# GDN chunk matrices kept in SBUF from preparation to merge, and the second half of the retention's gate columns moved behind the z columns

## The chip, the cores and the metric

The kernel runs on one core of one Trainium2 chip. The metric is the device time of one execution in microseconds (us). The number compared is the median over several runs of each kernel.

## The reference, cut to what matters

One layer of a hybrid block over 1280 tokens (256 context, 1024 latent, width 1024), all in 32-bit floats: modulated RMSNorm, one input projection, two head groups side by side, an output projection, a SwiGLU, a final norm. The part that the change touches:

```python
p = (h @ w_in)                                   # columns: q,k,v (GDN) | z | a,b | rq rk rv rg (retention)
qkv_a = silu(short_conv(qkv_a, conv_w))          # 5 taps, centred
q, k  = l2_normalize(q) * HEAD_DIM**-0.5, l2_normalize(k)
# gated delta rule (GDN), forward and backward, per chunk:
A     = where(strict, einsum('id,jd->ij', kb, kc) * decay, 0)
sol   = triangular_solve(A + I, rhs, lower, unit_diagonal)
qk    = einsum('id,jd->ij', qc, kc) * decay
...
o_gdn = rms_norm(o_f + o_b, gdn_norm_g) * silu(z)
o_ret = head_group_norm(r_f + r_b, ret_norm_g) * silu(rg)
```

The two parts changed are the way in which A's inverse is formed (its tiles are called the chunk matrices here), and the place in the program of half of the product that gives `rg`.

## The kernel before, in words

Every product of the input projection is done three times in a split form (high times high, high times low, low times high). Two forms of it matter here.

- *Token-major products* (`token_major(g, ...)`, tile `tm`, lines 371 to 373): group `g` is 256 columns of weights, 8 tiles of 128 latent tokens, and 8 x 3 matmuls of 128x256 for each tile, so 192 matmuls for a group. Groups 6 and 7 are the two halves of the gate columns `rg`, 8 and 9 those of `z`. A finish on ScalarE (`res`, line 532) makes silu of each bank and a DMA stores it to DRAM (`rd` or `zd`).
- *Convolution blocks* (`conv_block`, tile `b`, lines 605 to 607): 128 columns of q, k or v of one head, in chunks of 512 tokens of 24 matmuls each (and one of 256 for context). ScalarE copies a chunk out twice (`u`, and `y` at line 609); VectorE adds the other four taps (line 615); ScalarE applies silu (line 618).

Around the change the program goes as follows. The four k blocks come first, then norms: on VectorE a chain of small operations ends in `Gr` (line 671), which TensorE turns (`GT`, line 673), and which goes to DRAM as `grow_d`. Then come four q blocks (`qstat`, tile `qt`, turns each), and in the first two of them `ada_rest(5, half)`: a chain of eight VectorE operations over four loads of weights (`acc`, lines 497 and 499), one matmul `gr` (line 504), and one addition (`row`, line 505). Groups 6 and 7 of the token-major product follow, from the pool W2.

Then the GDN preparation. Ten tiles of 128 tokens go in three batches of 4, 4 and 2. `pre(t)` forms k.k (`kk`, line 724) and k.q (`kq`, 729) on TensorE; for each direction it loads a row of decays to all partitions (`gw`), GpSimd masks it (line 736), ScalarE takes four exponentials (740), and VectorE multiplies (`ut` at 744, `sp` at 746). `ut` goes to DRAM (`un`). `invert(b)` reads the 32x32 diagonal blocks back from `un` (`yr`, line 763), and solves all blocks of the batch at once on VectorE with 31 pairs of operations (lines 777 and 779, on `L`, `X` and `tmp`), then turns the result (`XT`, 781) and stores it to DRAM (`xd`). `merge(b)` loads the whole batch of matrices (`U`, line 795, from `un`) and puts the inverted blocks over its diagonal (799) and into `t` (800); TensorE then grows the blocks from 32 to 64 to 128 (tiles `m`, lines 819 to 846).

In program text the order is: solve(0), solve(1), four v blocks (tile `vT`, line 868, turns them; `vt` is stored to `sd`), the preparation of batch 2, merge(0), the load of the table `rope`, invert(2), merge(1), merge(2), and groups 8 and 9. Program text is not the order on the engines: a scheduler sets one order for each engine, with its own estimate of durations and with what the pools' buffers allow, and each engine runs its list strictly in that order. SyncE's queue (SP), which issues most loads and stores, has such a list too, and a transfer that must wait holds all that are behind it. Any edit to buffers or text can so reorder all engines.

Of the kernel before, what the change touches and what calls it, by code (L numbers as in the profile page):

```python
# [8 lines left out]
F32 = mybir.dt.float32  # L9
# [3 lines left out]
ALU = mybir.AluOpType  # L13
# [4 lines left out]
P = 128  # L18
# [4 lines left out]
NTOK = NCTX + NLAT  # L23
TT = NTOK // P
LT = NLAT // P
H = 4
# [12 lines left out]
def build(nc, tc, ap, dbg=None, stop=None, marks=None):  # L39
    root = ExitStack()  # L40
    V, S, G, T, SY = nc.vector, nc.scalar, nc.gpsimd, nc.tensor, nc.sync
# [149 lines left out]
    try:  # L191
# [426 lines left out]
            S.activation(y[:, a0:], y[:, a0:], AF.Silu)  # L618

        def newy():  # L620
            return CV.tile([P, NTOK], F32, tag="y", name="y", bufs=3)

        a4, b4, kds4, neG4 = (sm[n].rearrange("p (t d h) -> p t d h", d=2, h=4) for n in ("ab", "beta", "kds", "neG"))

# [78 lines left out]
        checkpoint("q")  # L703
        token_major(6, LAT, fin_gate, S, W2, SY)
        qstat(H - 1, qys[H - 1])
        token_major(7, LAT, fin_gate, S, W2, SY)
        checkpoint("rg")
        close(R2)
        close(W2)
# [4 lines left out]
        BATCH = [[0,1,2,9],[3,8,4,7],[5,6]]  # L714
        where = {t: (b, c) for b, ch in enumerate(BATCH) for c, t in enumerate(ch)}

        un = [dr.tile([P, 2, len(ch) * H, P], F32, tag="un%d" % b, name="un%d" % b) for b, ch in enumerate(BATCH)]

        def pre(t):
            b, c = where[t]  # L720
            kc = load(GP, kd[t], "kc", 2)
            pk = bank_b("kk")
            for h in range(H):
                T.matmul(pk[:, h * P:(h + 1) * P], kc[:, h, :], kc[:, h, :], start=True, stop=True)
            if t >= 2:
                qc = load(GP, qd[t - 2], "qc", 2)
                pq = bank_b("kq")
                for h in range(H):
                    T.matmul(pq[:, h * P:(h + 1) * P], kc[:, h, :], qc[:, h, :], start=True, stop=True)
            for d in range(2):  # L730
                gw = GP.tile([P, H, P], F32, tag="gw", name="gw", bufs=2)
                SY.dma_start(gw.rearrange("p h i -> p (h i)"),
                             grow_d[c8(t, d), :].rearrange("a b -> (a b)").partition_broadcast(P))
                e = GP.tile([P, H, P], F32, tag="e", name="e", bufs=2)
                sg = 1 if d == 0 else -1
                G.affine_select(out=e, in_=gw, compare_op=ALU.is_ge, fill=FAR, base=0,
                                pattern=[[0, H], [sg, P]], channel_multiplier=-sg)
                for h in range(H):
                    col = t * 8 + d * 4 + h
                    S.activation(e[:, h, :], e[:, h, :], AF.Exp, bias=sm["nG"][:, col:col + 1])  # L740
                if t >= 2:
                    sp = GP.tile([P, H, P], F32, tag="sp", name="sp", bufs=2)
                ut = GU.tile([P, H, P], F32, tag="ut", name="ut", bufs=2)
                V.tensor_tensor(ut.rearrange("p h i -> p (h i)"), pk, e.rearrange("p h i -> p (h i)"), ALU.mult)
                if t >= 2:
                    V.tensor_tensor(sp.rearrange("p h i -> p (h i)"), pq, e.rearrange("p h i -> p (h i)"), ALU.mult)
                SY.dma_start(un[b][:, 1 - d, c * H:(c + 1) * H, :], ut)
                if t >= 2:
                    SY.dma_start(sd[t, :, 8 - 8 * d], sp.rearrange("p h i -> p (h i)"))

# [4 lines left out]
        def invert(b):  # L755

            nc_ = len(BATCH[b])
            nu = nc_ * H
            nb = 4 * nu
            xd = xds[b] = dr.tile([4 * nb, 1024], F32, tag="xd%d" % b, name="xd%d" % b)  # L760
            yr = GI.tile([P, 1024], F32, tag="yr", name="yr", bufs=1)
            for k in range(4):
                SY.dma_start(yr[k:2 * nb:4].rearrange("r (i j) -> r i j", j=32),
                             un[b][q32[k]].rearrange("i e u j -> (e u) i j")[:, :, q32[k]])
            L = GI.tile([P, 1024], F32, tag="L", name="L", bufs=3)
            X = GI.tile([P, 1024], F32, tag="X", name="X", bufs=2)
            G.memset(X, 0.0)
            G.memset(X[:, 0::33], 1.0)
            m = lambda t: t[:2 * nb].rearrange("p (i j) -> p i j", j=32)
            S.activation(L[:nb], yr[:nb], AF.Copy)  # L770
            V.tensor_copy(m(L)[nb:], yr[nb:2 * nb].rearrange("p (i j) -> p j i", j=32))
            for j in range(31):
                n = 31 - j
                tmp = GI.tile([P, 256], F32, tag="tmp%d" % b, name="tmp", bufs=2)
                t3 = tmp[:2 * nb, :n * (j + 1)].rearrange("p (i c) -> p i c", c=j + 1)
                sh = [2 * nb, n, j + 1]
                V.tensor_tensor(t3, bc(m(L)[:, j + 1:, j], sh, 2), bc(m(X)[:, j, :j + 1], sh, 1), ALU.mult)
                xs = m(X)[:, j + 1:, :j + 1]
                V.tensor_tensor(xs, xs, t3, ALU.subtract)
            XT = GI.tile([P, 1024], F32, tag="L", name="XT", bufs=3)  # L780
            V.tensor_copy(m(XT), X[:2 * nb].rearrange("p (i j) -> p j i", j=32))
            for i, x in enumerate((X[:nb], XT[nb:2 * nb], X[nb:2 * nb], XT[:nb])):
                SY.dma_start(xd[i * nb:(i + 1) * nb], x)

        def blocks(b):

            nu = len(BATCH[b]) * H
            nb = 4 * nu

            def blk(dram, k):  # L790
                return dram.rearrange("(u b) (i j) -> b i u j", b=4, j=32)[k]

            at = G2 if b == 1 else GM
            uu = at.tile([P, 2, len(BATCH[b]), H, P], F32, tag="U", name="U%d" % b, bufs=1)
            SY.dma_start(uu.rearrange("p e c h j -> p e (c h) j"), un[b])
            tt = at.tile([P, 2, nu, 64], F32, tag="t64", name="t64", bufs=1)
            G.memset(tt, 0.0)
            for k in range(4):
                SY.dma_start(uu[q32[k]].rearrange("p e c h j -> p (e c h) j")[:, :, q32[k]], blk(xds[b][:2 * nb], k))
                SY.dma_start(tt[q32[k]].rearrange("p e u j -> p (e u) j")[:, :, (k % 2) * 32:(k % 2) * 32 + 32],  # L800
                             blk(xds[b][2 * nb:], k))
            return uu, [uu[:, 1 - d] for d in range(2)], [tt[:, d] for d in range(2)]

        def merge(b):
# [11 lines left out]
            for n in range(nu):  # L816
                for d, p, a, bb in pairs:
                    ca = (a % 2) * 32
                    T.matmul(ps1[q[bb], n * 32:n * 32 + 32], u[d][q[a], n, q[bb]], t[d][q[a], n, ca:ca + 32],
                             start=True, stop=True)  # L820
            xt1 = GM.tile([P, 16, 32], F32, tag="xt1", name="xt1", bufs=1)
            V.tensor_scalar(xt1.rearrange("p n j -> p (n j)")[:, :nu * 32], ps1[:, :nu * 32], -1.0, None, ALU.mult)
            ps2, ps3 = bank_b("m1"), bank_b("m1")
            for n in range(nu):
# [11 lines left out]
            halves = [(0, slice(0, 64), slice(64, 128)), (1, slice(64, 128), slice(0, 64))]  # L836
            for n0 in range(0, nu, 8):
                ps1, ps2 = bank_b("m2"), bank_b("m2")
                xt2 = GM.tile([P, 8, 64], F32, tag="xt2", name="xt2", bufs=1)
                for n in range(8):  # L840
                    for d, A, B in halves:
                        T.matmul(ps1[B, n * 64:n * 64 + 64], u[d][A, n0 + n, B], t[d][A, n0 + n, :], start=True, stop=True)
# [31 lines left out]
        RP = pool("rp", side="right")  # L874
        rope = RP.tile([P, TT, P], F32, tag="rope", name="rope")
        GM = pool("gm", side="right")
        for t in BATCH[2]:
            pre(t)
        close(GP)
# [7 lines left out]
        merge(2)  # L887


        for g in (8, 9):  # L890
            token_major(g, LAT, fin_gate, S, W)
        checkpoint("rgz")
        close(GM)
# [779 lines left out]
```

## Time and profile before

| | us |
|---|---|
| Median of 3 runs | 1485.98 (1479.36, 1485.98, 1486.84) |
| The profiled execution, own time | 1482.3 |
| Its span in the profile | 1480.4 |
| PE (TensorE matmuls) busy | 1399.8 (95%) |
| DVE (VectorE) busy | 981.1 (66%) |
| ACT (ScalarE) busy | 610.5 (41%) |
| POOL (GpSimd) busy | 579.5 (39%) |

The profile shows one execution. "Busy" sums the time in which an engine has an instruction running. PE lacks 80.6 us of the span; the stretch of 40 equal slices shows most of that between 300 and 470 us, and between 600 and 740 us. The stretch that the change touches is 195 to 480 us. The mean granted TensorE clock is 0.981 of full.

In the views, PE is TensorE's matmuls, PEld its weight loads, SP the SyncE queue. "out<-in" names tiles; a bracket at a row's end is the idle time of the engine ahead of it and what ended it. A row of the table by windows has the window, its length, then for PE, PEld, DVE, ACT and POOL the busy time and the count of instructions, then the granted TensorE clock, the mean busy share of the 16 DMA engines, and GB/s.

### The profile page before, as it was taken

What the parts mean: (1) busy time and instruction counts of PE and PEld (TensorE: products, weight loads), DVE (VectorE), ACT (ScalarE), POOL (GpSimd) and SP (SyncE); (2) the same over time, 40 slices, a digit from 0 to 9 for tenths busy, and PEclk for the clock granted to TensorE, in tenths of its full rate; (3) what the DMA queues carried; (4) which work ended last, traced back from release to release, by engine and by line L of the source; (5) the groups of instructions that cost most, each with busy time, mean ns of one, the idle gap of its engine ahead of it and who ended that gap; (6) DMA issues with size and microseconds to landing.
All of it is one profiled execution on the core that took longest, in us unless ns stands there. A gap on an engine that the chain in (4) does not pass through costs nothing.

```text
span 1480.4 us, 24179 instructions
## 1 busy us (share of the span) xinstructions
PE 1399.8 (95%) x8919; PEld 1200.6 (81%) x8919; DVE 981.1 (66%) x1909; ACT 610.5 (41%) x1336; POOL 579.5 (39%) x493
## 2 busy tenths in 40 slices
PE   7999999997889999998799899999999999999997
PEld 2798888876879999898588688877888888788886
DVE  6568797379772535789677886746555554657586
ACT  5543554765222111446444533323333333454454
POOL 0130010220102353254135588999555553335321
PEclk9999999999899999999799999999999999999999
DMA  9537686696878625985633265765232242786863
GB/s 338 186 104 230 178 245 204 199 297 191 256 193 272 247 69 185 411 328 181 217 115 115 85 215 210 266 240 178 107 107 107 107 150 74 239 279 195 306 202 114
DMA packets 170710, 293.95 MB, mean 199 GB/s; under 512 B 43528, under 2 KB 93912, under 8 KB 166496
## 3 DMA queue, kind: packets, MB, share of 16 engines
q1 hardware_dynamic: 119040, 248.98, 49.3%
q10 hardware_dynamic: 49072, 35.83, 7.7%
q0 software_dynamic: 2480, 7.60, 1.4%
q8 instruction: 70, 1.15, 0.3%
q14 instruction: 48, 0.39, 0.1%
HBM read 206.60 MB, written 85.77 MB: 197 GB/s over the span
## 4 chain that ended last, share of the span: by engine, by line
PE 40%; POOL 6%; DMA 2%; issue 1%; DVE 1%; ACT 0%; POOLq 0%; DVEq 0%; ACTq 0%
PE ffn L1362 7%; PE ffn L1360 6%; PE ffn L1361 6%; PE fo L1486 5%; PE fo L1488 5%; PE fo L1487 5%; DMA wd<-tw 2%; PE op L1219 2%; PE op L1220 2%; PE op L1221 2%; POOL ws L1333 1%; POOL tw L1414 1%; POOL tw L1413 1%; POOL tw L1416 1%; POOL tw L1415 1%
## 5 line engine op out<-in xcount | busy, mean ns | idle before, releaser
L371 PE MATMUL tm<-whi,hhi 128*128 128x256 f32 (+1 forms) x704 | 200.8, 290 | 7.2 <-ACT res L532 3.6
L372 PE MATMUL tm<-wlo,hhi 128*128 128x256 f32 (+1 forms) x704 | 200.4, 287 | 1.3 <-DVE wlo L345 1.3
L373 PE MATMUL tm<-whi,hlo 128*128 128x256 f32 (+1 forms) x704 | 198.7, 287 | 0.0
L371 PEld LDWEIGHTS tm<-whi,hhi 128*128 128x128 f32 x704 | 133.9, 192 | 11.5 <-ACT res L532 4.0
L1360 PE MATMUL ffn<-t,whi 128*128 128x512 f32 x352 | 136.9, 390 | 1.3 <-ACT whi L344 1.3
L1362 PE MATMUL ffn<-t,wlo 128*128 128x512 f32 x352 | 137.0, 390 | 0.8 <-DVE wlo L345 0.8
L372 PEld LDWEIGHTS tm<-wlo,hhi 128*128 128x128 f32 x704 | 134.9, 192 | 3.1 <-DVE wlo L345 1.7
L1361 PE MATMUL ffn<-t,whi 128*128 128x512 f32 x352 | 137.0, 389 | 0.0
L344 ACT ACTIVATE whi<-wraw 128x512 fp32r<-128x512 f32 (+2 forms) x98 | 75.1, 770 | 147.9 <-PE ffn L1361 81.9
L373 PEld LDWEIGHTS tm<-whi,hlo 128*128 128x128 f32 x704 | 134.2, 192 | 0.6 <-DVE hlo L314 0.2
L344 ACT ACTIVATE whi<-ws 128x512 fp32r<-128x512 f32 x88 | 55.6, 632 | 172.5 <-PE ffn L1361 131.3
L345 DVE TENSOR_TENSOR wlo<-ws,whi 128x512 fp32r<-128x512 f32 x88 | 94.0, 1069 | 46.5 <-ACT whi L344 46.3
L1486 PE MATMUL fo<-whi,ahi 128*128 128x512 f32 x308 | 119.3, 389 | 0.7 <-ACT ahi L344 0.7
L1487 PE MATMUL fo<-wlo,ahi 128*128 128x512 f32 x308 | 119.9, 389 | 0.0
L1488 PE MATMUL fo<-whi,alo 128*128 128x512 f32 x308 | 119.0, 390 | 0.0
L345 DVE TENSOR_TENSOR wlo<-wraw,whi 128x512 fp32r<-128x512 f32 (+2 forms) x92 | 100.7, 1097 | 23.4 <-ACT whi L344 23.4
L1360 PE MATMUL ffn<-b,whi 128*128 128x512 f32 x264 | 104.1, 394 | 4.1 <-ACT whi L344 4.1
L1362 PE MATMUL ffn<-b,wlo 128*128 128x512 f32 x264 | 103.9, 393 | 0.7 <-DVE wlo L345 0.7
L1361 PE MATMUL ffn<-b,whi 128*128 128x512 f32 x264 | 103.7, 393 | 0.0
L605 PE MATMUL b<-hhi,whi 128*128 128x512 f32 (+1 forms) x256 | 94.7, 370 | 0.8 <-ACT y L609 0.8
L607 PE MATMUL b<-hhi,wlo 128*128 128x512 f32 (+1 forms) x256 | 94.6, 370 | 0.0
L606 PE MATMUL b<-hlo,whi 128*128 128x512 f32 (+1 forms) x256 | 93.8, 366 | 0.0
(451 smaller groups left out, 3422.0 us busy)
## 6 DMA issues: line engine op xcount, KB each, us to landing
adaw<-ada SPq DMA_DIRECT2D x48, 512.0 KB, 4.6
pk<-sd SPq DMA_DIRECT2D x16, 1536.0 KB, 15.1
wraw<-wfi SPq DMA_DIRECT2D x44, 512.0 KB, 4.5
ar<-ad SPq DMA_DIRECT2D x33, 512.0 KB, 4.4
w<-wfo SPq DMA_DIRECT2D x22, 512.0 KB, 3.6
wd<-tw SPq DMA_DIRECT2D x11, 1024.0 KB, 4.9
ad<-act SPq DMA_DIRECT2D x20, 512.0 KB, 3.2
raw<-wd SPq DMA_DIRECT2D x20, 512.0 KB, 4.8
```

Source lines behind the costliest of these rows:

```text
L344: S.activation(hi, raw, AF.Copy)
L345: e.tensor_tensor(lo, raw, hi.bitcast(F32), ALU.subtract)
L371: T.matmul(o, hhi[:, k, tsl], whi[:, k % 4, :], start=(k == 0), stop=False)
L372: T.matmul(o, hhi[:, k, tsl], wlo[:, k % 4, :], start=False, stop=False)
L373: T.matmul(o, hlo[:, k, tsl], whi[:, k % 4, :], start=False, stop=(k == KT - 1))
L605: T.matmul(o, whi[:, k, :], hh, start=(k == 0), stop=False)
L1360: T.matmul(o, whi[:, k, :], xhi(xn, slice(0, 4), k), start=(first and k == 0), stop=False, **kw)
L1361: T.matmul(o, whi[:, k, :], xlo(xn, slice(0, 4), k), start=False, stop=False, **kw)
L1362: T.matmul(o, wlo[:, k, :], xhi(xn, slice(0, 4), k), start=False, stop=(k == 3), **kw)
L1486: T.matmul(po[g][i], ahi[:, ts], whi, start=(j == 0 and not kw), stop=False, **kw)
L1487: T.matmul(po[g][i], ahi[:, ts], wlo, start=False, stop=False, **kw)
L1488: T.matmul(po[g][i], alo[:, ts], whi, start=False, stop=(j == FH - 1), **kw)
```

## The change

- The products of k.k and the decays are written straight into SBUF tiles `us[b]` (`U0` and `U1` in the pool GU, `U2` in GM), in which `merge` then works. The 20 stores `un<-ut` of 256 KB and the three loads `U<-un` (2, 2 and 1 MB) are gone.
- The diagonal blocks go from `us[b]` to a small DRAM tensor `yd` in four transfers, and come back in one load `yr<-yd`; before they came by four loads out of `un`.
- `token_major(7, ...)` moves from behind `qstat` of the last head to the loop at the end, as `for g in (8, 9, 7)`, and takes its weights from the pool W in place of W2.
- Buffers: `y` 3 to 2, `gw` 2 to 3, the tile `e` is gone (the decays are masked and raised in place in `gw`), `L` 3 to 2, `X` 2 to 1, `tmp` shared and single, `xt1` and `xt2` share one buffer.

```diff
-            return CV.tile([P, NTOK], F32, tag="y", name="y", bufs=3)
+            return CV.tile([P, NTOK], F32, tag="y", name="y", bufs=2)
...
         qstat(H - 1, qys[H - 1])
-        token_major(7, LAT, fin_gate, S, W2, SY)
...
-        un = [dr.tile([P, 2, len(ch) * H, P], F32, tag="un%d" % b, name="un%d" % b) for b, ch in enumerate(BATCH)]
+        yd = [dr.tile([2 * len(ch) * H, 4, 32, 32], F32, tag="yd%d" % b, name="yd%d" % b) for b, ch in enumerate(BATCH)]
+        def matrices(b, pl):
+            return pl.tile([P, 2, len(BATCH[b]), H, P], F32, tag="U%d" % b, name="U%d" % b, bufs=1)
+        us = [matrices(b, GU) for b in range(2)]
...
-                gw = GP.tile([P, H, P], F32, tag="gw", name="gw", bufs=2)
+                gw = GP.tile([P, H, P], F32, tag="gw", name="gw", bufs=3)
-                e = GP.tile([P, H, P], F32, tag="e", name="e", bufs=2)
+                e = gw
...
-                ut = GU.tile([P, H, P], F32, tag="ut", name="ut", bufs=2)
-                V.tensor_tensor(ut.rearrange("p h i -> p (h i)"), pk, e.rearrange("p h i -> p (h i)"), ALU.mult)
+                V.tensor_tensor(us[b][:, 1 - d, c].rearrange("p h i -> p (h i)"), pk, e.rearrange("p h i -> p (h i)"), ALU.mult)
-                SY.dma_start(un[b][:, 1 - d, c * H:(c + 1) * H, :], ut)
...
-                SY.dma_start(yr[k:2 * nb:4].rearrange("r (i j) -> r i j", j=32),
-                             un[b][q32[k]].rearrange("i e u j -> (e u) i j")[:, :, q32[k]])
-            L = GI.tile([P, 1024], F32, tag="L", name="L", bufs=3)
-            X = GI.tile([P, 1024], F32, tag="X", name="X", bufs=2)
+                SY.dma_start(yd[b][:, k].rearrange("u i j -> i u j"),
+                             us[b][q32[k]].rearrange("p e c h j -> p (e c h) j")[:, :, q32[k]])
+            SY.dma_start(yr[:2 * nb], yd[b].rearrange("u k i j -> (u k) (i j)"))
+            L = GI.tile([P, 1024], F32, tag="L", name="L", bufs=2)
+            X = GI.tile([P, 1024], F32, tag="X", name="X", bufs=1)
-                tmp = GI.tile([P, 256], F32, tag="tmp%d" % b, name="tmp", bufs=2)
+                tmp = GI.tile([P, 256], F32, tag="tmp", name="tmp", bufs=1)
...
-            uu = at.tile([P, 2, len(BATCH[b]), H, P], F32, tag="U", name="U%d" % b, bufs=1)
-            SY.dma_start(uu.rearrange("p e c h j -> p e (c h) j"), un[b])
+            uu = us[b]
...
+        us.append(matrices(2, GM))
         for t in BATCH[2]:
             pre(t)
...
-        for g in (8, 9):
+        for g in (8, 9, 7):
             token_major(g, LAT, fin_gate, S, W)
```

The first place where the order changes is TensorE around `GT` and `gr`. Before, `tm` is the token-major product (groups 6 and 7), and rows like the last three go on, 97 in all, until the second `gr`:

```order
L673 MATMUL GT<-ident,Gr 80x128
L504 MATMUL gr<-acc,ones 1x512
L371 MATMUL tm<-whi,hhi 128x256
L372 MATMUL tm<-wlo,hhi 128x256
L373 MATMUL tm<-whi,hlo 128x256
```

After, at the same place, `b_2373` being the last chunk of the third q block, and `b_2432` the first of the fourth:

```order
L605 MATMUL b_2373<-hhi,whi 128x512
L606 MATMUL b_2373<-hlo,whi 128x512
L607 MATMUL b_2373<-hhi,wlo 128x512
L673 MATMUL GT<-ident,Gr 80x128
L504 MATMUL gr<-acc,ones 1x512 x2
L686 MATMUL qt<-ident,y 128x128 x16
L605 MATMUL b_2432<-hhi,whi 128x512
```

The two `gr` now stand one behind the other, without a token-major product between them; the fourth q block and the first v block have moved ahead of the first `kk`. Before, the fourth q block stood ahead of `GT`, and was followed by 51 token-major matmuls.

The second place is VectorE at the same point. Before, with two low halves of weights (`wlo`) in the chain of the second `acc`:

```order
L505 TENSOR_TENSOR row<-row,gr 1x512
L497 TENSOR_SCALAR acc<-adaw_2297,csl 128x512
L345 TENSOR_TENSOR wlo<-wraw,whi 128x1024
L499 SCALAR_TENSOR_TENSOR acc<-adaw_2297,csl,acc 128x512
L345 TENSOR_TENSOR wlo<-wraw,whi 128x1024
L499 SCALAR_TENSOR_TENSOR acc<-adaw_2301,csl,acc 128x512 x2
```

After, the chain stands by itself, and the taps of the q blocks (12 in a row, of which the first rows are shown) follow its end:

```order
L505 TENSOR_TENSOR row<-row,gr 1x512
L497 TENSOR_SCALAR acc<-adaw_2297,csl 128x512
L499 SCALAR_TENSOR_TENSOR acc<-adaw_2297,csl,acc 128x512
L499 SCALAR_TENSOR_TENSOR acc<-adaw_2301,csl,acc 128x512 x2
L499 SCALAR_TENSOR_TENSOR acc<-adaw_2305,csl,acc 128x512 x2
L499 SCALAR_TENSOR_TENSOR acc<-adaw_2309,csl,acc 128x512 x2
L505 TENSOR_TENSOR row<-row,gr 1x512
L615 SCALAR_TENSOR_TENSOR y<-u,cw,y 128x1022
```

The third place is the SP queue at the end of the preparation. Before, nothing of the first inversion stood behind the load of `rope`; only the loads of merge(0) did:

```order
L783 DMA xd_3172<-X 64x1024 x2
L783 DMA xd_3172<-XT 64x1024 x2
L763 DMA yr<-un_3013 16x32x32 x4
L795 DMA U_4162<-un_3011 128x4096
L883 DMA rope<-rope 128x1280
L800 DMA t_4164<-xd_3172 32x32x32 x4
L799 DMA U_4162<-xd_3172 32x32x32 x4
```

After, the last `gw` of the preparation stands behind `rope`, and so do the stores of the inversion (`xd`):

```order
L767 DMA yr<-yd_2776 128x1024
L751 DMA sd<-sp 128x512 x3
L886 DMA rope<-rope 128x1280
L736 DMA gw<-grow_d 128x512
L765 DMA yd_2777<-U_3786 32x16x32 x2
L751 DMA sd<-sp 128x512
```

The fourth place is VectorE at the end of the first inversion after the change: the last product of batch 2 (`U_3786`, which reads that last `gw`) stands between the inversion's last steps:

```order
L780 TENSOR_TENSOR tmp<-L,X 128x112
L747 TENSOR_TENSOR U_3786<-kk,gw 128x512
L749 TENSOR_TENSOR sp<-kq,gw 128x512
L782 TENSOR_TENSOR X<-X,tmp 128x4x28
L780 TENSOR_TENSOR tmp<-L,X 128x87
```

Before, all products of batch 2 stood further ahead, and nothing stood between the inversion's last steps and its turn `XT`:

```order
L746 TENSOR_TENSOR sp<-kq,e 128x512
L615 SCALAR_TENSOR_TENSOR y<-u,cw,y 128x1022
L777 TENSOR_TENSOR tmp<-L,X 128x135
L779 TENSOR_TENSOR X<-X,tmp 128x5x27
L777 TENSOR_TENSOR tmp<-L,X 128x112
L779 TENSOR_TENSOR X<-X,tmp 128x4x28
```

In the last part of the order on TensorE, 192 token-major matmuls (the first z group) stand behind the last `vT` and ahead of the first `m`, as before (191); the other two groups, 384 matmuls, are spread among the merges where 192 were.

More of the change, by code (lines that the diff above doesn't have):

```diff
@@ L779, in invert @@
                 V.tensor_tensor(xs, xs, t3, ALU.subtract)
-            XT = GI.tile([P, 1024], F32, tag="L", name="XT", bufs=3)
+            XT = GI.tile([P, 1024], F32, tag="L", name="XT", bufs=2)
             V.tensor_copy(m(XT), X[:2 * nb].rearrange("p (i j) -> p j i", j=32))
@@ L820, in merge @@
                              start=True, stop=True)
[L821 removed]
+            xt1 = GM.tile([P, 16, 32], F32, tag="xt", name="xt1", bufs=1)
             V.tensor_scalar(xt1.rearrange("p n j -> p (n j)")[:, :nu * 32], ps1[:, :nu * 32], -1.0, None, ALU.mult)
@@ L838, in merge @@
                 ps1, ps2 = bank_b("m2"), bank_b("m2")
-                xt2 = GM.tile([P, 8, 64], F32, tag="xt2", name="xt2", bufs=1)
+                xt2 = GM.tile([P, 8, 64], F32, tag="xt", name="xt2", bufs=1)
                 for n in range(8):
```

## The prediction

> **What bounds the kernel now.** I read the page first, then TensorE's waits between 195 and 480 us, then the table by windows, and last the timelines of the engines that TensorE waits for. The page's first row:
>
> ```profile
> PE 1399.8 (95%) x8919; PEld 1200.6 (81%) x8919; DVE 981.1 (66%) x1909; ACT 610.5 (41%) x1336; POOL 579.5 (39%) x493
> ```
>
> TensorE is the bound. The change takes no matmul away and adds none, so it can move the end only through TensorE's idle time (80.6 us of the span) and through its clock. The waits of TensorE from 195 to 480 us (total, times, longest):
>
> ```profile
> PE vT L868 <- ACT y L618: 13.1, 3, 11.5
> PE m L829 <- issue: 4.5, 2, 3.4
> PE tm L371 <- ACT res L532: 3.6, 2, 2.7
> ```
>
> The same stretch by windows:
>
> ```profile
> 240.00:250.00 10.00, 9.20 (x70) 7.94 (x69) 7.20 (x16) 6.79 (x17) 2.42 (x1) 1.00 0.84 237
> ...
> 280.00:300.00 20.00, 17.95 (x113) 15.63 (x112) 8.78 (x15) 12.12 (x39) 4.64 (x9) 1.00 0.88 296
> 300.00:320.00 20.00, 18.49 (x109) 15.58 (x109) 16.49 (x26) 12.76 (x27) 4.66 (x5) 1.00 0.96 303
> 320.00:340.00 20.00, 18.37 (x106) 15.76 (x105) 17.73 (x30) 14.16 (x36) 5.27 (x5) 1.00 0.90 308
> ...
> 360.00:370.00 10.00, 1.10 (x10) 0.91 (x9) 9.45 (x14) 6.08 (x12) 2.20 (x2) 0.82 0.70 223
> 370.00:380.00 10.00, 7.36 (x47) 7.36 (x48) 9.11 (x27) 3.19 (x4) 1.81 (x1) 0.67 0.96 341
> ...
> 390.00:400.00 10.00, 7.25 (x48) 7.05 (x48) 5.71 (x15) 1.50 (x4) 0.00 (x0) 0.83 0.86 209
> 400.00:410.00 10.00, 9.49 (x247) 8.73 (x247) 5.78 (x15) 3.83 (x5) 0.00 (x0) 1.00 0.76 170
> 410.00:420.00 10.00, 5.98 (x150) 5.77 (x150) 8.53 (x24) 3.81 (x7) 0.00 (x0) 0.71 0.79 196
> ```
>
> There are three kinds of hole. One is a thin spread of 5.2 us from 280 to 340 (20 less 17.95, 18.49 and 18.37). One is the hole of 11.5 us ahead of the last `vT`, in which VectorE is full (9.45 of 10). Then come the small holes among the merges: after 390, 2.75 + 0.51 + 4.02 = 7.3 us in these three windows, and slow clock in two of them: (1 - 0.83) x 10 + (1 - 0.71) x 10 = 4.6 us. Before the preparation, TensorE is nearly full: 0.8 us lost in 240 to 250.
>
> **Part 1, group 7 leaves the place behind `GT`.** The price of a token-major matmul, from the `tm` rows of the table by windows:
>
> ```profile
> 250.00:260.00 10.00, 9.85 (x84) 9.65 (x82) 0.00 (x0) 1.15 (x3) 1.00 0.45 146
> ```
>
> This is 9.85/84 = 0.117 us, and the group has 192: 22.5 us that TensorE does elsewhere. What it covered here is read from VectorE's timeline:
>
> ```profile
> 243.65 0.24 DVE L671 TENSOR_TENSOR Gr<-G,lna 128x80 f32<-128x80 f32 x1
> ...
> 247.13 0.67 DVE L505 TENSOR_TENSOR row<-row,gr 1x512 f32<-1x512 f32 x1 [0.66 <-PE gr L504]
> ...
> 248.13 1.21 DVE L345 TENSOR_TENSOR wlo<-wraw,whi 128x1024 fp32r<-128x1024 f32 x1
> ...
> 253.79 1.54 DVE L499 SCALAR_TENSOR_TENSOR acc<-adaw,csl,acc 128x512 f32<-128x512 f32 x2 [1.21 <-DMA adaw<-ada]
> 255.97 1.54 DVE L499 SCALAR_TENSOR_TENSOR acc<-adaw,csl,acc 128x512 f32<-128x512 f32 x2 [0.65 <-DMA adaw<-ada]
> 260.84 0.68 DVE L505 TENSOR_TENSOR row<-row,gr 1x512 f32<-1x512 f32 x1 [3.33 <-PE gr L504]
> ```
>
> From one `row` to the next are 13.7 us. Of these VectorE waited 3.3 for TensorE, which was busy with group 7, and spent 2.4 on two `wlo`; 8.0 us remain for the chain of the second `acc`. In the new order the second `gr` stands directly behind the first. The two need the one buffer of `acc`, so this whole chain is now a hole on TensorE, at least 8.0 - 1.9 = 6.1 us (if both loads of `adaw` are early) and at most 8.0 + 2; I take 8.0. Queued behind it on TensorE are the `qt`, the fourth q block and the first v block.
>
> How long TensorE waits for `GT` goes by what moved. The fourth q block (two chunks) now stands behind it. TensorE's timeline gives the chunk's price, and more that is needed below:
>
> ```profile
> 357.15 0.40 PE L606 MATMUL b<-hlo,whi 128*128 128x512 f32 x1
> 357.38 0.39 PE L607 MATMUL b<-hhi,wlo 128*128 128x512 f32 x1
> ...
> 372.64 2.40 PE L868 MATMUL vT<-ident,y 128*128 128x128 f32 x10 [11.54 <-ACT y L618]
> ...
> 376.12 0.41 PE L371 MATMUL tm<-whi,hhi 128*128 128x256 f32 x1
> 376.33 0.40 PE L372 MATMUL tm<-wlo,hhi 128*128 128x256 f32 x1
> ...
> 377.05 0.28 PE L371 MATMUL tm<-whi,hhi 128*128 128x256 f32 x1
> 377.17 0.28 PE L372 MATMUL tm<-wlo,hhi 128*128 128x256 f32 x1
> ```
>
> A convolution matmul takes 0.23 us, a chunk of 24 5.5 us, two chunks 11 us. Ahead of `GT` stand 9 token-major matmuls more than before (1 us), so TensorE comes to it 10 us earlier, at about 236. `Gr` on VectorE comes earlier only by the taps that now run behind it, four operations of 1.2 us less one `wlo`: about 239.5. That is a hole of 3.4 us (0 if `Gr` is earlier still, 6 if its chain does not move).
>
> Then the buffers: with two `y` in place of three, the fourth q block's `y` needs the first `qt` of an earlier head, and its first copies run behind the 12 taps that VectorE has saved up. I allow 2.5 us (0 to 5; the bounds are nothing, and four taps of 1.2).
>
> The clock is the last item here. After the hole of 11.5 us the matmuls follow at 0.21 us (376.12 to 376.33), and from about 376.7 at 0.12; so after 372.64 some 4 us passed at about half speed, 2 us lost. Windows 390 to 400 and 410 to 420 lost 1.7 and 2.9 with smaller holes. I take 2 us for the 8 us hole and nothing for the two small ones. [...]
>
> Taken off is the 0.8 us hole that stood there. Part 1: +8.0 + 3.4 + 2.5 + 2 - 0.8 = +15.1 us.
>
> **Part 2, the convolution blocks ahead of the preparation.** The first v block and the fourth q block now precede the first `kk`, and the matmuls `kk` and `kq` are spread among the later chunks, so the preparation's waits (mask, exponentials, store of `ut`) have more matmuls above them. Of the 5.2 us from 280 to 340 I take 3 as gone (0 to 5.2). VectorE loses nothing by the removed stores: 20 products stay, at the same size.
>
> **Part 3, the hole ahead of the last `vT` stays.** VectorE's timeline around its end:
>
> ```profile
> 370.01 1.28 DVE L615 SCALAR_TENSOR_TENSOR y<-u,cw,y 128x1022 f32<-128x1022 f32 x1
> ...
> 374.01 1.14 DVE L781 COPY XT<-X 128x1024 f32<-128x1024 f32 x1
> ```
>
> The last matmul of the last v block starts at 357.4, and its last tap ends 371.3, 13.9 us later. In the new order 21 steps of the inversion are moved behind that tap, which gives VectorE about 7 us; but the v blocks also come sooner. I take 1.5 us off the hole (0 to 5). No token-major matmul stands ahead of that `vT`, so group 7 does not fill it.
>
> **Part 4, group 7 among the merges.** Here it can fill holes: at most the 7.3 us and 4.6 us of clock above. But merge(0) itself becomes late. The queue of SyncE, and the stores of `vt` on ScalarE's queue with their landing times:
>
> ```profile
> 370.63 0.32 SPq L795 DMA_DIRECT2D U<-un  x1
> ...
> 383.18 0.32 SPq L795 DMA_DIRECT2D U<-un  x1
> 392.32 0.34 SPq L883 DMA_DIRECT2D rope<-rope  x1
> 392.76 5.03 SPq L800 DMA_DIRECT2D t<-xd  x4
> 397.83 4.35 SPq L799 DMA_DIRECT2D U<-xd  x4
> ...
> L871 ACTq DMA_DIRECT2D sd<-vt x9: 366/367/465, 347.2 to 383.2; - x9
> ...
> DMA to landing us min/median/max: 1.9/3.0/7.6
> ```
>
> `rope` goes out only when the last store of `vt` has landed: 21 us after the last tap. Before, it held up 9 us of loads of merge(0) (383.2 to 392.3). Now the last `gw` stands behind it, and the product that reads that `gw` stands on VectorE ahead of the inversion's last seven steps. I take the release of `rope` 10 us after the last tap (8 to 21: the 4 MB of `U` no longer compete with those stores, and the last store is issued 383.2 - 371.3 = 12 us after the tap at the latest). Then come the load of `gw`, mask, exponentials, product and the last steps, another 10 us by the times of such rows. So `XT` is ready 20 us after the tap, where it took 2.7 us before (374.01). From `XT` to merge(0) the stores and loads take 16 us (two rows of 5.03 and 4.35 us, and landings). TensorE has 22.5 us of the first z group to do from about 4 us after the tap, and some microseconds of slow clock: it is through 28 to 30 us after the tap, and merge(0) is ready at 36. So a hole of 5 us replaces the ones of before, and with some 3 us more at merge(1) and in the clock, 8 of the 12 us remain: -4 us (-11 to +9).
>
> The 10 MB of stores and loads of `un` that fall away cost TensorE nothing where they were, since no row of its waits names them; I count 0. The diagonal blocks take as many hops as before (store, then load).
>
> **The sum.** +15.1 - 3 - 1.5 - 4 = +6.6 us against the profiled execution's 1482.3: 1489. That execution lies 3.7 us below the median of the runs, 1486, so the comparison would show about +0.3 to +0.5%. I predict 1490. The runs differ by 7.5 us, 0.5%, and less than that can't be told from no change.
>
> **The rivals.**
>
> 1. *Group 7 fills the merges, and the hole at `gr` is small.* It needs the `adaw` loads early and `Gr` earlier (6.1 us and 0 for 8.0 and 3.4, no wait for `y`), all of 280 to 340 filled, the hole at `vT` shrunk by 4, and all 12 us among the merges gone. That gives 6.1 + 1 - 0.8 - 5.2 - 4 - 11 = -14, 1468. For it speaks that a whole group is more matmul time than all those holes; against it, that most of the new cover stands behind merge(0).
> 2. *Slower: the last `gw` behind `rope`.* If `rope` waits the full 21 us after the last tap as it did before, `XT` is ready at 31 and merge(0) at 47, 11 us later than I took, with no matmul to put in that place: 1489 + 11 + 2 of clock = 1502. It decides as soon as the stores of `vt` land later than about 10 us after the tap; each microsecond beyond is one of the end. For it speaks the row of `rope` above; against it, that 2 MB of `U` left just ahead of those stores.
> 3. *The change does nothing*: the holes at `GT` and `gr` (13.9 us without clock) are paid back by the thin spread, the `vT` hole and the merges, all near their better ends: 1482 to 1488.
>
> **How the numbers follow.** My sum and rival 3 lie within 0.5% for the most part: 0.42 together. Rival 1 has 0.22. Rival 2 and the sum with the poorer ends of part 1 (+4 and more) have 0.36. The range goes from near rival 1 to rival 2, 1470 to 1503; the likeliest case alone, 1480 to 1497.
>
> **What would show it.** In the profile after: a hole of about 8 us on TensorE ending in the second `gr`, waiting for `acc` L499, and one of 3 us at `GT`; a hole of about 10 us at the last `vT`, for `y` L618; token-major rows running past the end of the first merge; `XT` some 20 us behind the last tap L615, with `gw` behind `rope` in between. I am wrong if the `gr` hole is under 4 us, or if `XT` comes within 10 us of the tap (then 1480 or less), or if `rope` again waits 20 us (then 1500 and more).

## The result, and the profile after

| | before | after |
|---|---|---|
| Median, us | 1485.91 (1479.36 to 1486.84) | 1498.50 (1496.49 to 1503.91) |
| Ratio to before, 95% interval | 1 | 1.0113 (1.0087 to 1.0139) |
| Profiled execution, own time | 1482.3 | 1499.8 |
| Its span | 1480.4 | 1498.0 |
| PE busy | 1399.8 | 1406.1 |
| PE idle (span less busy) | 80.6 | 91.9 |

The change makes the kernel 1.1% slower by the measured ratio, about 17 us, and 17.6 us by the spans of the two profiles; the two medians in the table lie nearer, 12.6 us. Ratios are used from here on. The time lies in the range given (1470 to 1503), but the forecast called "within 0.5%" the likeliest, and that was not so.

The page's first row of the kernel after, then TensorE's waits between 195 and 500 us:

```profile
PE 1406.1 (94%) x8919; PEld 1204.3 (80%) x8919; DVE 974.1 (65%) x1909; ACT 615.4 (41%) x1340; POOL 580.9 (39%) x493
```

```profile
PE vT L870 <- ACT y L618: 9.7, 2, 8.5
PE gr L504 <- DVE acc L499: 9.5, 1, 9.5
PE m L821 <- DMA t<-xd: 8.9, 4, 3.3
PE kq L733 <- issue: 6.0, 2, 3.4
PE GT L673 <- DVE lnb L677: 4.1, 1, 4.1
```

The same matmuls ran (8919 in both). Of the 17.6 us of span, 11.3 are more idle time on TensorE. The other 6.3 are busy time of the same instructions: the mean granted clock is 0.974, and was 0.981, and by an estimate from two windows (in "The clock", below) 3.8 us of them are slow clock. The table by windows, with the columns of the prediction, first after, then before:

```profile
200.00:240.00 40.00, 35.91 (x209) 31.10 (x207) 32.91 (x89) 20.03 (x62) 2.37 (x1) 0.99 0.76 233
240.00:300.00 60.00, 50.43 (x261) 40.40 (x261) 34.12 (x40) 33.74 (x114) 13.14 (x11) 0.86 0.47 143
300.00:340.00 40.00, 31.37 (x199) 27.31 (x198) 24.82 (x45) 27.51 (x59) 7.94 (x9) 0.98 0.75 225
340.00:380.00 40.00, 31.46 (x200) 29.02 (x200) 34.55 (x64) 22.32 (x41) 8.58 (x7) 0.85 0.66 193
380.00:500.00 120.00, 109.82 (x1815) 104.82 (x1814) 67.73 (x174) 32.75 (x61) 11.93 (x23) 0.97 0.67 188
```

```profile
200.00:240.00 40.00, 40.00 (x201) 33.39 (x200) 35.85 (x85) 19.89 (x61) 2.41 (x1) 1.00 0.76 231
240.00:300.00 60.00, 56.33 (x420) 51.54 (x419) 28.70 (x43) 37.17 (x132) 11.57 (x15) 1.00 0.67 209
300.00:340.00 40.00, 36.85 (x213) 31.33 (x213) 34.22 (x56) 26.91 (x62) 9.93 (x10) 1.00 0.93 305
340.00:380.00 40.00, 27.55 (x168) 24.82 (x168) 38.08 (x78) 19.70 (x33) 4.01 (x3) 0.87 0.64 198
380.00:500.00 120.00, 109.75 (x1824) 105.62 (x1822) 66.78 (x176) 30.99 (x56) 19.15 (x34) 0.96 0.79 237
```

Idle time is the window's length less the number behind it: 4.1, 9.6, 8.6, 8.5 and 10.2 us after, and 0, 3.7, 3.1, 12.4 and 10.2 before. So there are two new losses, at 235 to 255 (the place of `GT` and `gr`) and at 300 to 340 (the preparation). One hole shrank, ahead of the last `vT`. The merges lost as much as before, although some 180 more token-major matmuls stand between the first `m` and the last (510, where 329 stood).

### The profile page after: what moved, and what is told of

Same layout as the page of the kernel before. It is cut to its first block, busy times and chain, and to the rows that moved or that the text cites. A ratio compares the mean times of both kernels' runs of the same rounds, so it can differ in the third digit from the quotient of the medians.

```text
span 1498.0 us, 24150 instructions
## 1 busy us (share of the span) xinstructions
PE 1406.1 (94%) x8919; PEld 1204.3 (80%) x8919; DVE 974.1 (65%) x1909; ACT 615.4 (41%) x1340; POOL 580.9 (39%) x493
## 4 chain that ended last, share of the span: by engine, by line
PE 40%; POOL 6%; DMA 2%; issue 1%; DVE 1%; ACT 0%; SPq 0%; POOLq 0%; DVEq 0%; ACTq 0%
PE ffn L1365 6%; PE ffn L1363 6%; PE ffn L1364 6%; PE fo L1489 5%; PE fo L1491 5%; PE fo L1490 5%; PE op L1222 2%; PE op L1224 2%; PE op L1223 2%; DMA wd<-tw 2%; POOL ws L1336 1%; POOL tw L1417 1%; POOL tw L1419 1%; POOL tw L1416 1%; POOL tw L1418 1%
## 6 DMA issues: line engine op xcount, KB each, us to landing
pk<-sd SPq DMA_DIRECT2D x16, 1536.0 KB, 13.6
```

## The experiments

Theory A: the loss is the cover that group 7 gave to `GT` and `gr`. Theory B: it is what the SBUF path brought with it (two `y`, the in-place `gw`, the single `X`). Each kernel was timed against the kernel before on the same chip. "Idle, 300 to 340" is TensorE's, from the table by windows. "Wait for gw" is GpSimd's total wait for loads of `gw` between 280 and 420 us, from its waits.

| kernel | ratio to before (95%) | idle, 300 to 340 | wait for gw |
|---|---|---|---|
| after | 1.0113 (1.0087 to 1.0139) | 8.6 | 61.7 |
| sbuf_only | 1.0049 (1.0032 to 1.0066) | 5.2 | 52.6 |
| g7_only | 1.0077 (1.0062 to 1.0093) | 3.9 | 20.3 |
| acc_late | 1.0078 (1.0061 to 1.0095) | 4.0 | 43.9 |
| rope_late | 1.0092 (1.0070 to 1.0114) | 7.1 | 44.3 |
| products_late | 1.0114 (1.0096 to 1.0132) | 8.2 | 27.5 |
| gw_five | 1.0095 (1.0081 to 1.0108) | 1.5 | 42.5 |
| all_three | 1.0142 (1.0128 to 1.0157) | 11.6 | 55.9 |
| y_two | 0.9958 (0.9946 to 0.9969) | 7.3 | 19.7 |
| y2_gw_in_place | 1.0166 (1.0144 to 1.0188) | 8.5 | 64.5 |
| y2_x_single | 1.0056 (1.0036 to 1.0076) | 5.2 | 13.2 |
| sbuf_gw_five | 1.0028 (1.0013 to 1.0043) | 2.6 | 45.5 |
| y2_deep | 0.9951 (0.9933 to 0.9969) | 4.7 | 11.5 |

Neither of the last two columns sets the time by itself: products_late waits 27.5 us for `gw`, less than half of the changed kernel's 61.7, and takes as long; gw_five has the fewest idle microseconds from 300 to 340, and y_two is faster with 7.3.

**sbuf_only**: the changed kernel with group 7 back in its old place.

```diff
         qstat(H - 1, qys[H - 1])
+        token_major(7, LAT, fin_gate, S, W2, SY)
...
-        for g in (8, 9, 7):
+        for g in (8, 9):
```

> The changed kernel with group 7 put back behind the last qstat (weights from W2), all else as changed: matrices in SBUF, y 2, X 1. On TensorE 72 token-major matmuls stand ahead of GT again and 96 between the two gr; from the first kk on the order is that of the changed kernel less 192 token-major matmuls among the merges. Theory A (the loss is the cover that group 7 gave to GT and gr: holes of 4.1 and 9.5 us and some 3.5 us of slow clock, which the merges did not pay back): 17 us come off at GT and gr, the merges lose some cover (0 to 8 us): 1482 to 1490. Theory B (the loss comes from the SBUF path and its narrower buffers: y 2, X 1, the last gw behind rope): 1495 to 1499.

Measured 1490.61 us, 1.0049. The holes at `GT` and `gr` are gone (no idle time from 200 to 300), and 0.6% of the 1.1% with them. But 0.5% stays: the time lies just above A's 1482 to 1490 and below B's 1495 to 1499, and neither alone explains the loss.

**g7_only**: the kernel before, with group 7 moved alone.

```diff
-        token_major(7, LAT, fin_gate, S, W2, SY)
...
-        for g in (8, 9):
+        for g in (8, 9, 7):
```

> The kernel before with only group 7 moved behind the z groups; the matrices still go through DRAM, y 3, X 2. Group 6's matmuls stand ahead of GT (72), but only 9 between the two gr. Theory A: a hole of about 7 us at gr plus 2 to 3 of clock, less what the merges can use of the group (233 matmuls ahead of the first merge, gain 0 to 8): 1487 to 1495, slower than before. Theory B: no loss, 1478 to 1486.

Measured 1493.86 us, 1.0077. Its waits on TensorE show the hole, and the one at the last `vT`, which the group does not reach:

```profile
PE vT L867 <- ACT y L618: 10.9, 2, 10.3
PE gr L504 <- DVE acc L499: 8.3, 1, 8.3
```

The move costs without the SBUF path too. A holds for this part of the loss.

**acc_late**: the second chain of `acc` in the fourth q block in place of the second.

```diff
-            if h < 2:
-                ada_rest(5, h)
+            if h in (0, 3):
+                ada_rest(5, h // 3)
```

> The changed kernel with ada_rest(5, 1) moved in the text from the second to the fourth q block. The first gr still stands behind GT, the second now stands behind the fourth q block's two chunks and 6 matmuls of the first v block (about 12 us of matmuls). Theory A: the hole of 9.5 us at gr and about 3 us of slow clock go, the 4.1 us at GT stays: 1485 to 1489. Theory B: under 3 us, 1495 to 1499.

Measured 1493.17 us, 1.0078. The wait of `gr` is gone. But only some 5 us come back ((1.0113 - 1.0078) x 1483), about half of what A expected, so both expectations missed. In the profile TensorE's idle time falls by 8.8 us (91.9 to 83.1), but PE busy rises by 3.1, to 1409.2, where 3 us of slow clock were to go: from 280 to 300 the granted clock is now 0.86 (1.00 in the changed kernel), beside 3.2 us of idle time that were not there. Among the merges (380 to 500) it is idle for 10.4 us (10.2 in the changed kernel).

**rope_late**: `rope` queued behind the loads of the first merge.

```diff
-        SY.dma_start(rope, ap["rope"])
+        with tc.issue_after(loads[0]):
+            SY.dma_start(rope, ap["rope"])
```

> The changed kernel with the load of rope queued on SP behind the loads of the first merge, so that the last gw does not stand behind it; the order of the rest is the same but for a few rows. If the last gw behind rope is what makes the first inversion end late (XT at 382.1, 18 us behind the last tap), that gw goes out some 6 us earlier, XT comes 4 us earlier, and so does the first merge, of whose holes (5 us from 390 to 410) 2 to 4 go: 1494 to 1496. Rival (the inversion's own 31 pairs of steps set XT, or the merge's loads do): no change, 1497 to 1499.

Measured 1497.43 us, 1.0092, not told apart from the changed kernel. The reason is in the queues. First SP and VectorE of the changed kernel, then of rope_late (both timelines, start and length):

```profile
371.77 0.33 SPq L886 DMA_DIRECT2D rope<-rope  x1
372.20 0.38 SPq L736 DMA_DIRECT2D gw<-grow_d  x1
```

```profile
363.05 1.28 DVE L615 SCALAR_TENSOR_TENSOR y<-u,cw,y 128x1022 f32<-128x1022 f32 x1
...
370.78 1.88 DVE L747 TENSOR_TENSOR U<-kk,gw 128x512 f32<-128x512 f32 x3
379.05 0.69 DVE L747 TENSOR_TENSOR U<-kk,gw 128x512 f32<-128x512 f32 x1 [2.89 <-ACT gw L744]
382.08 1.14 DVE L784 COPY XT<-X 128x1024 f32<-128x1024 f32 x1
```

```profile
372.99 0.32 SPq L736 DMA_DIRECT2D gw<-grow_d  x1
```

```profile
372.24 1.88 DVE L747 TENSOR_TENSOR U<-kk,gw 128x512 f32<-128x512 f32 x3
379.02 0.69 DVE L747 TENSOR_TENSOR U<-kk,gw 128x512 f32<-128x512 f32 x1 [2.37 <-ACT gw L744]
382.91 1.13 DVE L784 COPY XT<-X 128x1024 f32<-128x1024 f32 x1
```

With `rope` out of the way, the last `gw` still goes out only at 372.99. It is the fourth of batch 2 and there are three buffers, so it takes the buffer of the first, whose product starts at 372.24. SP's own waits from 340 to 400 in rope_late name that product:

```profile
SPq L736 <- DVE U L747: 11.1, 1, 11.1
```

In the changed kernel `rope` and that product came at nearly the same time, and its trace alone did not tell them apart.

**products_late**: the products of batch 2 behind `XT`.

```diff
+                with tc.issue_after(xts2[0]) if b == 2 else nullcontext():
                     V.tensor_tensor(us[b][:, 1 - d, c]..., pk, e..., ALU.mult)
...
-            V.tensor_copy(m(XT), X[:2 * nb]...)
+            xts2[b] = V.tensor_copy(m(XT), X[:2 * nb]...).ins
```

> The changed kernel with one thing added: VectorE's products of batch 2 (U2, line 747) are queued behind XT of the first inversion, in place of between its last steps. Theory: with the matrices in SBUF and gw as their work buffer, the fourth gw of batch 2 can be loaded only when the first product of that batch is done, and the product that needs it stands ahead of the inversion's last seven steps; this, not rope, makes XT late (18 to 19 us behind the last tap in the changed kernel and in rope_late alike). Then XT comes 9 to 11 us behind the last tap, TensorE's wait for t<-xd (8.9 us) falls under 4 us, and 4 to 6 us go: ratio to the kernel before 1.006 to 1.009, where the changed kernel had 1.011. Rival: the merges wait for something else next (the next inversion, its stores and loads): XT is early, the time stays at 1.010 to 1.012.

Measured 1500.94 us, 1.0114: the rival. `XT` came at 376.8 in place of 382.1, and the wait for `t` fell, but TensorE waited at the next places among the merges:

```profile
PE m L824 <- DMA t<-xd: 5.0, 3, 2.7
...
PE m L831 <- issue: 4.2, 1, 4.2
PE tm L373 <- issue: 2.5, 1, 2.5
```

From 380 to 500 its idle time was 13.3 us (10.2 in the changed kernel). A late `XT` is real, but it is not the price. y_two, below, says the same: there `XT` comes at 383.0, 9 us later than in the kernel before (374.0), and that kernel is faster.

**gw_five**: five `gw`; the room is taken from the inversion.

```diff
-                gw = GP.tile([P, H, P], F32, tag="gw", name="gw", bufs=3)
+                gw = GP.tile([P, H, P], F32, tag="gw", name="gw", bufs=5)
...
-            L = GI.tile([P, 1024], F32, tag="L", name="L", bufs=2)
+            L = GI.tile([P, 1024], F32, tag="L", name="L", bufs=1)
...
-            XT = GI.tile([P, 1024], F32, tag="L", name="XT", bufs=2)
+            XT = GI.tile([P, 1024], F32, tag="yr", name="XT", bufs=1)
```

> The changed kernel with five gw buffers for three; the room comes from L (one buffer for two) and from XT, which takes yr's buffer, so the second inversion's diagonal blocks are loaded only after the first one's XT is stored. Theory: gw is now held from its load to the last product (before, mask and exponentials went into a second buffer, e, so that four were under way), and this is why TensorE's holes from 300 to 340 us grew from 3.1 to 8.6 us: they fall to 5 or less, and the products of batch 2 come earlier: ratio 1.006 to 1.009. Rival: the two y buffers or the SP queue make those holes: 7 to 9 us stay, ratio 1.010 or more.

Measured 1497.21 us, 1.0095. The holes went as the theory says, from 8.6 to 1.5 us, and `XT` came at 372.6; the time did not follow clearly (the intervals overlap). The deeper `gw` was paid for with a shallower inversion; y2_gw_in_place and y2_x_single, below, change the two apart.

**y_two**: the kernel before with two `y`, one line.

```diff
-            return CV.tile([P, NTOK], F32, tag="y", name="y", bufs=3)
+            return CV.tile([P, NTOK], F32, tag="y", name="y", bufs=2)
```

> The kernel before with two y buffers for three, nothing else. TensorE's order up to the first kk is that of sbuf_only, so against sbuf_only (1.0049) it separates the order that the two y make from the SBUF path. If the y buffers are the cost: 1.003 to 1.006, with the holes from 300 to 340 near 5 us. If the in-place gw, the single X and the late XT are the cost: 0.998 to 1.002, and holes near 3.

Measured 1477.38 us, 0.9958: faster than before, outside both expectations. Two `y` make the scheduler put the fourth q block and the first v block ahead of the first `kk`, with group 7 still behind `GT`; from 200 to 300 TensorE is never idle (3.7 us before). So two `y` are a gain, and what the rest of the SBUF path costs is 1.0049 against 0.9958, 0.9%. Where the gain comes from is not shown: over the whole span TensorE is idle as long as before (81.0 us, 80.6 before), since the preparation now has more holes (7.3 us from 300 to 340, 3.1 before), and it is PE busy that is shorter (1395.3, 1399.8 before).

**all_three**: acc_late and products_late together, and group 7 ahead of the last v block.

```diff
         for h in range(H):
             y = newy()
+            if h == 3:
+                token_major(7, LAT, fin_gate, S, W)
             conv_block(8 + h, y, False)
...
-        for g in (8, 9, 7):
+        for g in (8, 9):
```

> The changed kernel with three moves: ada_rest(5, 1) in the fourth q block (as in acc_late), the products of batch 2 behind XT (as in products_late), and group 7 in the text ahead of the last v block, so that its 192 matmuls stand between the third and the fourth v block. If the holes add up as read (gr 9.5 gone, the 8.5 us ahead of the last vT down to 3 to 5 because VectorE catches up during group 7, the wait for t<-xd gone): 17 us less than the changed kernel, ratio 0.998 to 1.002. If slow clock and the holes among the merges take it back: 1.004 to 1.008.

Measured 1504.26 us, 1.0142, the slowest but one and far outside both expectations. Its waits on TensorE:

```profile
PE vT L875 <- ACT y L618: 13.7, 2, 9.7
PE kq L735 <- issue: 12.0, 3, 4.9
```

The hole ahead of the last `vT` is no smaller (9.7), since the last taps run behind the last chunk wherever that stands. And the preparation now waits 12.0 us at `kq`, with 152 convolution matmuls between its first `kk` and its last `kq`, where the changed kernel has 221. Holes do not add up when the cover of one is taken from another.

**y2_gw_in_place**: y_two, with the mask and the exponentials in place in `gw`.

```diff
-                gw = GP.tile([P, H, P], F32, tag="gw", name="gw", bufs=2)
+                gw = GP.tile([P, H, P], F32, tag="gw", name="gw", bufs=3)
-                e = GP.tile([P, H, P], F32, tag="e", name="e", bufs=2)
+                e = gw
```

> y_two with one piece of the SBUF path: the mask and the exponentials work in place in gw (three buffers), no tile e; the matrices still go through DRAM. y_two had 0.996, sbuf_only 1.005. If the in-place gw is what the SBUF path costs: 1.001 to 1.005. If not: 0.994 to 0.998.

Measured 1508.25 us, 1.0166: this piece alone costs 2.1% against y_two, more than the whole change and more than either expectation. GpSimd's waits, first in the kernel before, then after, then in y_two, then in y2_gw_in_place (total, times, longest):

```profile
POOL e L736 <- DMA gw<-grow_d: 23.9, 5, 8.5
```

```profile
POOL gw L740 <- DMA gw<-grow_d: 61.7, 15, 16.4
```

```profile
POOL e L736 <- DMA gw<-grow_d: 19.7, 4, 6.1
```

```profile
POOL gw L736 <- DMA gw<-grow_d: 64.5, 13, 17.4
```

With a separate `e`, a `gw` is free as soon as GpSimd has masked it, and the next load is under way while exponentials and products run. In place, a `gw` is held until the last product, so each load starts late and its landing stands in the chain. GpSimd's waits show the late loads. That they are the whole price is not shown: from 306 us on, TensorE's order differs from y_two's too, and no run here keeps the order while it changes the buffers. Against y_two TensorE is idle 15.8 us longer (96.8 and 81.0) and busy 11.3 us longer. TensorE's waits in this kernel follow. The profile names no releaser for the first; that `kq` waits there for a bank that a late product has not freed is argued, not shown:

```profile
PE kq L729 <- issue: 13.8, 3, 5.7
PE vT L868 <- ACT y L618: 8.7, 2, 8.3
PE tm L371 <- ACT vt L870: 7.9, 1, 7.9
```

**y2_x_single**: y_two, with the inversion's buffers as in the change.

```diff
-            L = GI.tile([P, 1024], F32, tag="L", name="L", bufs=3)
-            X = GI.tile([P, 1024], F32, tag="X", name="X", bufs=2)
+            L = GI.tile([P, 1024], F32, tag="L", name="L", bufs=2)
+            X = GI.tile([P, 1024], F32, tag="X", name="X", bufs=1)
...
-                tmp = GI.tile([P, 256], F32, tag="tmp%d" % b, name="tmp", bufs=2)
+                tmp = GI.tile([P, 256], F32, tag="tmp", name="tmp", bufs=1)
...
-            XT = GI.tile([P, 1024], F32, tag="L", name="XT", bufs=3)
+            XT = GI.tile([P, 1024], F32, tag="L", name="XT", bufs=2)
```

> y_two with the other piece: X single, L two, one tmp for all batches; the matrices still go through DRAM, gw and e as before. The second inversion can then start only when the first one's X is stored (in the changed kernel VectorE waited 5.6 us there). If that is the cost of the SBUF path: 1.000 to 1.004. If the second inversion has that much slack: 0.994 to 0.998.

Measured 1490.45 us, 1.0056, 1.0% above y_two and above both expectations. TensorE's order up to the first merge is y_two's; among the merges, from 410 us on, it differs. VectorE waits ahead of an inversion until `X` of the one before is stored and GpSimd has cleared it again (its profiled execution was one of the longer ones, span 1496.2, so the size is rough):

```profile
DVE tmp L777 <- POOL X L768: 13.5, 2, 11.2
```

That this wait is what costs the 1.0% is argued, not shown: in this execution TensorE is idle only 3.8 us longer than in y_two's (84.8 and 81.0), and busy 16.1 us longer, at a mean granted clock of 0.974 (0.980 in y_two's).

**sbuf_gw_five**: sbuf_only with gw_five's edit.

> sbuf_only (matrices in SBUF, group 7 in its old place) with five gw buffers, the room taken from L and from XT as in gw_five. If the shallow gw is what the SBUF path costs, this comes from 1.005 to 0.996 to 1.000, and holes from 300 to 340 fall from 5.2 to under 3. If the cost is the single X or the round trip of the diagonal blocks: 1.003 to 1.007.

Measured 1487.42 us, 1.0028. The holes from 300 to 340 fall to 2.6 us, as the first expectation says, but the time stays just under the second one, and its interval overlaps that of sbuf_only. VectorE now waits for loads into `yr`, whose buffer `XT` shares; what this costs was not measured apart:

```profile
DVE L L775 <- DMA yr<-yd: 20.2, 3, 12.4
```

**y2_deep**: y_two with three `gw` and three `e`.

```diff
-                gw = GP.tile([P, H, P], F32, tag="gw", name="gw", bufs=2)
+                gw = GP.tile([P, H, P], F32, tag="gw", name="gw", bufs=3)
-                e = GP.tile([P, H, P], F32, tag="e", name="e", bufs=2)
+                e = GP.tile([P, H, P], F32, tag="e", name="e", bufs=3)
```

> y_two with three gw and three e (two each before): the room that the third y left goes to the preparation. y_two's holes on TensorE from 300 to 340 were 7.3 us. If the preparation is short of such buffers there: 3 us or more go, 0.991 to 0.995, the fastest so far. If the exponentials' engine or the loads set it: 0.995 to 0.997, as y_two.

Measured 1476.53 us, 0.9951, the fastest here, but not told apart from y_two. Both beat the kernel before and the changed one.

**What they add up to.** From before to after in three steps: two `y`, -0.42%; the rest of the SBUF path, +0.91% (sbuf_only against y_two); group 7's move, +0.64% (after against sbuf_only). They make the measured +1.13% by the way in which they are formed, so the sum is no test; g7_only is one, and has +0.77% for the same move. Within the middle step, the in-place `gw` costs +2.1% and the single `X` +1.0%, each measured alone on the DRAM path and each with the order that its edit brings. Their sum is more than 0.91%, so if they add up, keeping the matrices in SBUF itself gains about 2%; that was not measured alone, nor were the trip of the diagonal blocks through `yd` and the shared buffer of `xt1` and `xt2`, and all_three shows that such sums can fail.

## Why the prediction was right or wrong

| term, us | predicted | in the profile after |
|---|---|---|
| Part 1, hole at `gr` | +8.0 | +9.5 |
| Part 1, hole at `GT` | +3.4 | +4.1 |
| Part 1, wait of `y` | +2.5 | about 0 (200 to 260 idle 13.7, of which the two holes are 13.6) |
| Part 1, taken off | -0.8 | -1.6 (200 to 280 before) |
| Part 2, preparation (280 to 340) | -3 | +3.4 |
| Part 3, ahead of the last `vT` | -1.5 | -3.0 |
| Part 4, merges (380 to 500), idle | -4 with clock | 0.0 |
| clock at the `gr` hole | +2 | about +4 there (PE busy +6.3 in all) |

**Part 1 was right**, but for the wait of `y`, which did not come. TensorE's timeline shows both holes as forecast:

```profile
239.80 0.40 PE L673 MATMUL GT<-ident,Gr 128*80 128x128 f32 x1 [4.09 <-DVE lnb L677]
240.14 1.86 PE L504 MATMUL gr<-acc,ones 128*1 128x512 f32 x2
251.46 1.86 PE L504 MATMUL gr<-acc,ones 128*1 128x512 f32 x2 [9.46 <-DVE acc L499]
```

Reading the chain of `acc` between two `row` in VectorE's timeline, and seeing in the order that nothing else stood there, was enough.

**Part 2 was the step that failed**, in two ways. First, it reckoned that the preparation's waits would "have more matmuls above them". They have fewer: 221 convolution matmuls stand between the first `kk` and the last `kq`, where 288 stood before, since a block that moves ahead of the first `kk` covers nothing behind it. In y_two, where nothing but `y` was edited, there are 221 as well, and the idle time from 300 to 340 is 7.3 us (3.1 before). Second, the sum wrote that "VectorE loses nothing by the removed stores". It priced the stores, and did not price the buffers that were changed beside them: `e = gw`, and `X` from 2 to 1, had no term at all. On the DRAM path those edits cost +2.1% and +1.0%. In the holes of TensorE the miss is 6.4 us (from -3 to +3.4). How it divides between the two stays open: sbuf_only has all of those buffers, and is idle for 5.2 us from 300 to 340.

**Part 3** had the right sign, and the hole stayed, as said; it shrank by 3.0 us, not by 1.5.

**Part 4** was too hopeful, and its mechanism was wrong. `XT` came 17.8 us behind the last tap (382.08 less 364.3), where 20 were forecast, and the last `gw` did stand behind `rope`. But `rope` was not what held it: rope_late moved `rope`, and `XT` stayed, since the fourth `gw` waited for a buffer. The two came free at nearly the same time, so it is luck that the number came out so near. products_late then brought `XT` forward, and nothing was won. The merges were idle for 10.2 us, as before, where 4 us were to go with the clock, and that with some 180 more matmuls in their order. The order fixes where those matmuls stand; in products_late the waits moved to the next `m`.

**The clock** was sized too small. The sum had 2 us for the hole at `gr` and nothing for the one at `GT`; the two windows of 10 us behind the latter, in which TensorE was busy for 2.0 and 8.4 us, show 0.50 and 0.67:

```profile
240.00:250.00 10.00, 2.00 (x3) 0.09 (x2) 6.01 (x10) 0.00 (x0) 1.41 (x2) 0.50 0.66 195
250.00:260.00 10.00, 8.43 (x32) 5.77 (x33) 4.56 (x6) 5.51 (x31) 1.17 (x1) 0.67 0.41 117
```

In these two windows the four `gr` took 1.01 to 1.06 us each, where they took 0.59 in the kernel before (first before, then after; least, median and greatest in ns):

```profile
L504 PE MATMUL gr<-acc,ones x4: 590/590/591, 246.1 to 260.2; 128*1 128x512 f32 x4
```

```profile
L504 PE MATMUL gr<-acc,ones x4: 1011/1034/1057, 240.1 to 252.3; 128*1 128x512 f32 x4
```

An estimate of the busy time lost in the two windows, from their rows, is the busy time by the share of the clock that was not granted: (1 - 0.50) x 2.0 + (1 - 0.67) x 8.4 = 3.8 us.

What the rest of the 6.3 us of busy time belongs to stays open.

Rival 1 did not come: none of its conditions held, neither the small hole at `gr`, nor the filled preparation, nor the filled merges. The time of rival 2 (1502) is near the one measured, but its mechanism is not the cause: `rope` went out 7.4 us behind the last tap, not 21. The upper end of the range was set by that rival, so that the time lies in the range is in part luck; the sum itself gave 1489 where the profiled execution took 1499.8.

## What to carry to other kernels

When an edit takes memory from one place to give it to another, price every buffer count that it touches as a term of the sum: ask how long each buffer is now held, and which load or store can start only when it is free. Working in place saves a tile and removes the stage of prefetch that the tile was: in y2_gw_in_place GpSimd waited 64.5 us for loads of `gw`, and 19.7 in y_two. And before moving a filler, list what stands in its old place: the hole that it leaves can be read off the order (8.0 and 3.4 us were forecast here, and 9.5 and 4.1 came), while the holes at the new place belong to a chain that may simply move (in products_late the wait for `t` fell from 8.9 to 5.0 us, and the time stayed). When blocks change sides of a stage, count the matmuls that are left beside it.

## What the runs showed that was not expected

One buffer fewer made the kernel faster: with two `y` for three, 0.42% (ratio 0.9946 to 0.9969). The scheduler then orders the convolution blocks in another way; what in that order is worth the 0.42% stays open. A count of buffers is an input to the order, too, and not only room. And the most costly piece of the change (2.1%) was one whose edit adds no instruction and no transfer: it delays the moment at which a load of 256 KB may start (GpSimd's longest wait for one was 17.4 us, and 6.1 in y_two), and changes the order with it.
